# An encoder block in fp32 on one core: the first half's index queries for 128 tokens, in plain fp32

## The chip, the cores and the metric

The kernel runs on one core of a Trainium2 chip. A core has a matrix engine (TensorE, PE in the profile; its weight loads are shown as PEld), a vector engine (VectorE, DVE), a scalar engine (ScalarE, ACT), GpSimd (POOL), a queue engine that only starts transfers (SyncE, SP) and 16 DMA engines. Each engine works through its own instructions in order; they wait for one another by semaphores. The metric is the device time of one execution in microseconds (us), less is better.

## The reference

One layer for 512 tokens of width 2048, in fp32: a normed input is projected by one wide matrix `w_in`, two attention branches run on parts of the projection, their gated sum is added to the input, and a mixture-of-experts step (PEER) follows. What matters here is the index branch. It decides for each token which keys the sparse attention (DSA) may look at:

```python
h = rmsnorm(x, norm_mix_g[l])
proj = jnp.einsum('bsd,de->bse', h, w_in[l])
c_q, c_kv, k_rope, dq, dk, dv, iq, ik, iw, gates = jnp.split(proj, splits, axis=-1)
...
q_idx = rope(q_idx.reshape(B, S, IDX_HEADS, IDX_DIM), positions, IDX_ROT)      # 16 heads of 64
k_idx = rope(k_idx[:, :, None, :], positions, IDX_ROT)[:, :, 0, :]
top_k = min(DSA_TOPK_MAX, S // 4)                                              # 128
# for each block of 128 queries:
dots = jnp.einsum('bqhd,bsd->bqhs', qi_blk, k_idx).astype(jnp.float32) * IDX_DIM ** -0.5
index_score = jnp.einsum('bqh,bqhs->bqs', w, jax.nn.relu(dots))
index_score = jnp.where(allowed[None], index_score, NEG_INF)
_, sel = lax.top_k(index_score, top_k)
```

The first block of 128 tokens sees at most 128 keys, so all of them are chosen, whatever its index scores are.

## The kernel before

The 512 tokens are worked in two halves of 256 columns (HB), each of two blocks of 128 (P). For each half, `projections` lays the input out as 16 slices of k (KT), [128 x 256] each, and makes the projection in output chunks of 128 rows; `attention`, `branches` and `residual` follow. The expert step for both halves comes after, with gathers on POOL and DVE running beside the second half. A scheduler orders the instructions of each engine beforehand, by program order, priorities (weight loads go first) and a simulated time line; on the chip the order is fixed.

Precision comes from splitting. `wload` brings a weight tile of 128x1024 from memory (`raw`, 4 buffers, on SP's queue), ACT rounds it to `hi` (L114) and DVE makes the rest `lo` (L115); the input stands as `hT` and `lT` alike (L435, L437). `mm3` (L140 to L142) makes one product in three matmuls: hi by hi, hi by lo, lo by hi. `xraw` brings a weight tile without splitting it, for plain fp32 matmuls; the second half already uses that for its upper eight slices (`hF`, L386).

`proj_chunk(m)` is one output chunk of 128 rows for the 256 tokens of the half: two weight tiles, 16 slices, 48 matmuls of 256 columns in the first half. `scaled` multiplies the result by the row norms `rrow` (L397). The order of chunks in a half is: one for the keys (W_KRIK), two gates, eight of index queries (W_IQ), six latent ones, ten for the sparse attention's keys and queries, thirty gates.

The norms come out of the same loop that fills hT: ACT squares each slice (L440), DVE adds them up (L442), PE sums over partitions (L466), DVE and ACT make the reciprocal root (L148 to L154). PE can work two chunks ahead, the `pm` buffers, before the first scaled result `xk` must be taken out.

Each chunk m of index queries holds two heads of 64 rows. It is scaled, turned by position (`rope_near`: a shuffle, two products and a sum on DVE), and split by `stacked`: two ACT casts into `two` (L347), a DVE subtraction into `cq[1]` (L348), and two small transfers on SP's queue (L349, L350) that put the lower parts into the other 64 partitions. `cq[0]` has slots for two chunks (m % 2), `cq[1]` for four (m % 4). For each head and each block in `looks` then come two score matmuls against the keys (L354, L355), a Relu on ACT (L511) and a weighted sum on DVE into `sel` (L512). `looks` leaves block 0 out, so in the first half only block 1 is scored, though queries are made for both blocks. `tick` and `between` pace the gathers and the expert search and do nothing in the first half.

Of the kernel before, what the change touches and what calls it, by code (L numbers as in the profile page):

```python
# [7 lines left out]
F32 = mybir.dt.float32  # L8
# [9 lines left out]
P = 128  # L18
S = 512
# [58 lines left out]
def emit(tc, a, out):  # L78
    nc = tc.nc
    R = dict(side="right")  # L80
    with ExitStack() as top:
# [36 lines left out]
        def xraw(src):  # L118
            with tc.high_priority():
                raw = wp.tile([P, 1024], F32, name="raw", tag="raw", bufs=4)[:, :flat(src)]  # L120
                nc.sync.dma_start(raw, src)
            return raw
# [209 lines left out]

        def rope_near(dst, src, cs, half, tp):

            sh = tp.tile([P, HB], F32, name="rt2", tag="rt2")
            nc.vector.stream_shuffle(sh, src, [i ^ half for i in range(32)])
            t1 = tp.tile([P, HB], F32, name="rt1", tag="rt1")
            nc.vector.tensor_mul(t1, src, cs[0])
            nc.vector.tensor_mul(sh, sh, cs[1])
            dst = sh if dst is None else dst  # L340
            nc.vector.tensor_add(dst, t1, sh)
            return dst

        def stacked(two, lo, src):

            for t in two:
                nc.scalar.copy(t, src)  # L347
            nc.vector.tensor_sub(lo, src, two[0].bitcast(F32))  # L348
            nc.sync.dma_start(two[0][64:, :].bitcast(F32), lo[:64, :].bitcast(F32))  # L349
            nc.sync.dma_start(two[1][:64, :].bitcast(F32), lo[64:, :].bitcast(F32))  # L350
# [9 lines left out]
        def projections(i, pj, own, between, tick):  # L360
# [4 lines left out]
            with ExitStack() as st:  # L365
# [3 lines left out]
                hT = hp.tile([P, ks, HB], F32R, name="hT")  # L369
                lT = hp.tile([P, ks, HB], F32R, name="lT")  # L370
                hF = hp.tile([P, KT - ks, HB], F32, name="hF") if ks < KT else None
                trig = hp.tile([P, 4, HB], F32, name="trig")
                rcol = hp.tile([P, 2], F32, name="rcol")
                rrow = hp.tile([P, HB], F32, name="rrow")
# [5 lines left out]
                def proj_chunk(m):  # L380
                    pm = ps.tile([P, S], F32, name="pm", tag="mm")[:, :HB]
                    for hf in range(2):
                        if 8 * hf >= ks:
                            w = xraw(a["win"][m, hf])
                            for j in range(8):
                                nc.tensor.matmul(pm, w[:, j * P:(j + 1) * P], hF[:, j, :], start=False, stop=j == 7)  # L386
                            continue
                        wh, wl = wload(a["win"][m, hf])
                        for j in range(8):
                            k = 8 * hf + j  # L390
                            mm3(pm, wh[:, j * P:(j + 1) * P], wl[:, j * P:(j + 1) * P],
                                hT[:, k, :], lT[:, k, :], k == 0, k == KT - 1)
                    between(m)
                    return pm

                def scaled(dst, pm):
                    tick(nc.vector.tensor_mul(dst, pm, rrow), 5.7)  # L397
                    return dst
# [27 lines left out]
                with tc.tile_pool(name=f"a{i}", bufs=1) as ap:  # L426
                    sq = dq[:, 3, :]
                    for k0, n in [(k, min(3, e - k)) for b_, e in ((0, ks), (ks, KT)) for k in range(b_, e, 3)]:
                        src = a["wdv"][:, k0 * 272:(k0 + n) * 272]
                        wh, wl = wload(src) if k0 < ks else (xraw(src), None)  # L430
                        for k in range(k0, k0 + n):
                            if k % 4 == 0:
                                xt = xraw(a["xt"][i, k // 4])
                            x_ = xt[:, (k % 4) * HB:(k % 4 + 1) * HB]
                            nc.scalar.activation(hT[:, k, :] if k < ks else hF[:, k - ks, :], x_, AF.Copy, scale=gmix[:, k:k + 1])  # L435
                            if k < ks:
                                nc.vector.scalar_tensor_tensor(lT[:, k, :], x_, gmix[:, k:k + 1], hT[:, k, :].bitcast(F32),  # L437
                                                               ALU.mult, ALU.subtract)
                            s2 = sq if k == 0 else dq[:, 4 + k % 4, :]
                            nc.scalar.activation(s2, x_, AF.Square)  # L440
                            if k:
                                nc.vector.tensor_add(sq, sq, s2)  # L442
                        if k0 == K_A:
                            if i == 0:
                                nc.sync.dma_start(fr, a["freq"])
                                nc.sync.dma_start(ident, a["cmat"][:, 0:P])
                            nc.sync.dma_start(kk.bitcast(I32), a["posr"][:, side])
                            nc.vector.tensor_copy(posf, kk.bitcast(I32))
                            angles(2)
                        for j, tb in enumerate(blocks):  # L450
                            ts_ = slice(j * P, (j + 1) * P)
                            for d_ in range(n):
                                k = k0 + d_
                                if k >= ks:
                                    nc.tensor.matmul(pd[j], hF[:, k - ks, ts_], wh[:, d_ * 272:(d_ + 1) * 272],
                                                     start=False, stop=k == KT - 1)
                                    continue
                                mm3(pd[j], hT[:, k, ts_], lT[:, k, ts_], wh[:, d_ * 272:(d_ + 1) * 272],
                                    wl[:, d_ * 272:(d_ + 1) * 272], k == 0, k == KT - 1)
                    if i == 0:  # L460
                        nc.sync.dma_start(cm, a["cmat"][:, P:6 * P].rearrange("p (j q) -> p j q", j=5))
                        nc.sync.dma_start(cmask, a["cmask"])
                        nc.sync.dma_start(gq, a["gqkv"])
                        nc.sync.dma_start(iota, a["iota"])
                    pr = ps.tile([P, S], F32, name="prr", tag="tr")[:, :HB]
                    nc.tensor.matmul(pr, ones, sq, start=True, stop=True)  # L466
                    rr = rstd_of(ap, pr, D, "r")
                    nc.vector.tensor_copy(rrow, rr)
                    for j in range(2):
                        dg = ap.tile([P, P], F32, name="dg")  # L470
                        nc.vector.tensor_mul(dg, rr[:, j * P:(j + 1) * P], ident)
                        nc.vector.tensor_reduce(rcol[:, j:j + 1], dg, AX.X, ALU.add)
                    for j, tb in enumerate(blocks):
                        rc = rcol[:, j:j + 1]
                        nc.scalar.copy(dvw[:, tb, :], pd[j])
                        nc.vector.tensor_scalar(dvw[:, tb, :256], dvw[:, tb, :256], rc, None, ALU.mult)
                        nc.vector.tensor_scalar(dvw[:, tb, 256:], dvw[:, tb, 256:], rc, 1.0 / 32.0, ALU.mult, ALU.mult)
# [14 lines left out]


                for m in range(8):
                    xi = tp.tile([P, HB], F32, name="xi")
                    scaled(xi, proj_chunk(W_IQ + m))
                    iq = rope_near(None, xi, cs[2], 8, tp)

                    two = [cq[0][:, 2 * (m % 2) + j, :] for j in range(2)]
                    stacked(two, cq[1][:, m % 4, :], iq)  # L500
                    for hh in range(2):
                        h = 2 * m + hh
                        for b in looks:
                            n = (b + 1) * P
                            qs = slice((b % 2) * P, (b % 2 + 1) * P)
                            pi = ps.tile([P, S], F32, name="pi", tag=("tr", "po")[turn[0] % 2])[:, :n]
                            mm_stacked(pi, two, hh, qs, *ik, n, True, True)
                            turn[0] += 1
                            o = 4 + 2 * (turn[0] % 2)
                            rl = dq[:, o:o + 2, :].rearrange("p h t -> p (h t)")[:, :n]  # L510
                            nc.scalar.activation(rl, pi, AF.Relu)  # L511
                            nc.vector.scalar_tensor_tensor(  # L512
                                sel[b], rl, dvw[:, b, 256 + h:257 + h], cmask[:, S - n:] if h == 0 else sel[b],
                                ALU.mult, ALU.add)
# [587 lines left out]
```

## Time and profile before

| | |
|---|---|
| time, median of 3 runs | 3625.94 us (3624.42 to 3628.35) |
| the profiled execution | 3632.17 us, span 3630.4 us |
| PE / PEld / DVE / ACT / POOL busy | 94% / 84% / 78% / 39% / 16% |
| mean granted TensorE clock | 0.972 |
| HBM traffic | 281 GB/s over the span |

The profile is of one execution; its times are from the start of the span. Busy times are unions, so two overlapping matmuls count once. [...]

### The profile page before, as it was taken

Reading aid. Unit: us, or ns where it says so; the run is one execution under the profiler, and the core shown is the slowest. Engines: PE = TensorE matmul, PEld = TensorE weight load, DVE = VectorE, ACT = ScalarE, POOL = GpSimd, SP = SyncE. Lnnn points to the kernel's source line nnn. Section 1 sums busy time; section 2 is a strip of 40 time slices with the busy share of each in tenths; the row PEclk is TensorE's granted clock in tenths of the full one; section 3 lists DMA queues with packets and bytes.
Section 4 is the critical chain, followed back from the end, with each engine's and each line's share of the span. In section 5 each row is a group of like instructions: output and inputs, shape, how many; then the busy total and the mean of one; then the engine's idle time right before and its main releaser. Section 6 shows DMA issues by size and latency. Waiting matters only on the chain.

```text
span 3630.4 us, 55449 instructions
## 1 busy us (share of the span) xinstructions
PE 3407.4 (94%) x20981; PEld 3054.9 (84%) x20981; DVE 2842.7 (78%) x4726; ACT 1434.0 (39%) x2171; POOL 595.6 (16%) x388
## 2 busy tenths in 40 slices
PE   8999999999889788879999999999999999999997
PEld 7999898777788678659999999998778787788786
DVE  7854565589998778768998787876878788789797
ACT  6444554543122353334345444453233223233233
POOL 0000000000112222220001111110322233233232
PEclk9999999999999999989999999999999999999999
DMA  6566357543799768876788988989989898999997
GB/s 200 171 199 204 110 172 241 163 161 122 279 366 389 275 235 300 338 281 217 263 295 303 333 333 321 335 324 332 344 318 350 311 349 332 356 353 348 348 351 285
DMA packets 282108, 1026.23 MB, mean 283 GB/s; under 512 B 29424, under 2 KB 98672, under 8 KB 228080
## 3 DMA queue, kind: packets, MB, share of 16 engines
q1 hardware_dynamic: 193136, 565.47, 45.0%
q0 software_dynamic: 55296, 402.68, 29.0%
q10 hardware_dynamic: 33408, 54.54, 4.0%
q8 instruction: 165, 2.70, 0.3%
q14 instruction: 103, 0.84, 0.1%
HBM read 960.71 MB, written 58.72 MB: 281 GB/s over the span
## 4 chain that ended last, share of the span: by engine, by line
PE 73%; DVE 11%; DMA 8%; issue 5%; ACT 2%; POOL 0%; SPq 0%; DVEq 0%; ACTq 0%; POOLq 0%
PE pv L141 8%; PE pv L142 8%; PE pv L140 8%; PE pu L142 6%; PE pu L140 6%; PE pu L141 6%; PE pm L140 5%; PE pm L142 5%; PE pm L141 5%; DVE r L269 3%; DMA gt<-g_d 2%; PE pg L877 2%; DVE lo L115 2%; PE pu L832 2%; DMA raw<-in_vd 1%
## 5 line engine op out<-in xcount | busy, mean ns | idle before, releaser
L114 ACT CAST hi<-raw 128x1024 fp32r<-128x1024 f32 (+1 forms) x852 | 889.9, 1048 | 1346.1 <-PE pv L142 296.8
L115 DVE TENSOR_TENSOR lo<-raw,hi 128x1024 fp32r<-128x1024 f32 (+1 forms) x852 | 1033.3, 1218 | 491.3 <-issue 124.4
L267 POOL DMA_INDIRECT r<-in_u,idx x256 | 366.3, 1431 | 2525.6 <-DVE dots L269 1406.7
L141 PE MATMUL pv<-lo,ch 128*128 128x512 f32 x1536 | 600.6, 394 | 24.3 <-DVE lo L115 24.3
L142 PE MATMUL pv<-hi,cl 128*128 128x512 f32 x1536 | 594.2, 393 | 0.0
L269 DVE CUSTOM_DVE_ANT_0 r<-r,h2g 128x2048 f32<-128x2048 f32 x256 | 582.4, 2284 | 11.0 <-DMA r<-in_u,idx 11.0
L140 PE MATMUL pv<-hi,ch 128*128 128x512 f32 x1536 | 540.6, 392 | 9.4 <-ACT hi L114 8.6
L140 PE MATMUL pu<-h2h,hi 128*128 128x256 f32 x1888 | 539.2, 286 | 8.2 <-ACT hi L114 8.2
L142 PE MATMUL pu<-h2h,lo 128*128 128x256 f32 x1888 | 532.6, 282 | 0.5 <-DVE lo L115 0.5
L141 PE MATMUL pu<-h2l,hi 128*128 128x256 f32 x1888 | 531.4, 282 | 0.0
L140 PE MATMUL pm<-hT,hi 128*128 128x256 f32 x1368 | 405.3, 296 | 28.6 <-DVE sg L397 16.5
L142 PE MATMUL pm<-hT,lo 128*128 128x256 f32 x1368 | 397.5, 291 | 9.8 <-DVE lo L115 9.7
L141 PE MATMUL pm<-lT,hi 128*128 128x256 f32 x1368 | 396.6, 290 | 0.0
L141 PEld LDWEIGHTS pv<-lo,ch 128*128 128x128 f32 x1536 | 292.0, 190 | 91.0 <-DVE lo L115 30.2
L140 PEld LDWEIGHTS pu<-h2h,hi 128*128 128x128 f32 x1888 | 357.4, 189 | 9.0 <-ACT hi L114 8.5
L141 PEld LDWEIGHTS pu<-h2l,hi 128*128 128x128 f32 x1888 | 357.5, 189 | 0.4
L142 PEld LDWEIGHTS pu<-h2h,lo 128*128 128x128 f32 x1888 | 356.8, 189 | 0.9 <-DVE lo L115 0.8
L140 PEld LDWEIGHTS pv<-hi,ch 128*128 128x128 f32 x1536 | 290.2, 189 | 72.0 <-ACT hi L114 10.3
L142 PEld LDWEIGHTS pv<-hi,cl 128*128 128x128 f32 x1536 | 291.7, 190 | 60.6
L280 POOL DMA_INDIRECT r<-in_v,idx x128 | 229.2, 1790 | 484.1 <-DVE hacc L282 396.4
L282 DVE SCALAR_TENSOR_TENSOR hacc<-r,dots,hacc 128x2048 f32<-128x2048 f32 x128 | 300.1, 2345 | 8.5 <-DMA r<-in_v,idx 8.4
L140 PEld LDWEIGHTS pm<-hT,hi 128*128 128x128 f32 x1368 | 266.7, 195 | 37.3 <-issue 21.5
(356 smaller groups left out, 5262.0 us busy)
## 6 DMA issues: line engine op xcount, KB each, us to landing
raw<-in_ut SPq DMA_DIRECT2D x256, 512.0 KB
raw<-in_vd SPq DMA_DIRECT2D x256, 512.0 KB
raw<-in_win SPq DMA_DIRECT2D x228, 512.0 KB
raw<-in_wbr SPq DMA_DIRECT2D x64, 512.0 KB
raw<-in_wo SPq DMA_DIRECT2D x64, 512.0 KB
g_d<-gs ACTq DMA_DIRECT2D x24, 1024.0 KB
gt<-g_d SPq DMA_DIRECT2D x8, 3072.0 KB
raw<-in_wq SPq DMA_DIRECT2D x32, 512.0 KB
```

Source lines behind the costliest of these rows:

```text
L114: nc.scalar.copy(hi, raw)
L115: latest[0] = nc.vector.tensor_sub(lo, raw, hi.bitcast(F32))
L140: nc.tensor.matmul(ps, wh, xh, start=first, stop=False)
L141: nc.tensor.matmul(ps, wh, xl, start=False, stop=False)
L142: nc.tensor.matmul(ps, wl, xh, start=False, stop=last)
L267: nc.gpsimd.indirect_dma_start(out=r, out_offset=None, in_=a["u"], in_offset=bass.IndirectOffsetOnAxis(ap=idx[b][:, j:j + 1], axis=0))
L269: nc.vector.tensor_tensor_reduce(out=r, in0=r, in1=h2g[b], scale=1.0, scalar=0.0, op0=ALU.mult, op1=ALU.add, accum_out=dots[b][:, j:j + 1])
L280: nc.gpsimd.indirect_dma_start(out=r, out_offset=None, in_=a["v"], in_offset=bass.IndirectOffsetOnAxis(ap=idx[0][:, j:j + 1], axis=0))
L282: nc.vector.scalar_tensor_tensor(acc, r, dots[0][:, j:j + 1], acc, ALU.mult, ALU.add)
L832: nc.tensor.matmul(pu, w[:, j * P:(j + 1) * P], h2f[:, j, :], start=False, stop=j == 7)
L877: end[0] = nc.tensor.matmul(pg[:, j], o2[:, j, :], og[:, j, :], start=True, stop=True)
```

## The change

In the first half (i = 0) the eight index-query chunks are made for block 1 alone. A new tile `h1` holds block 1's 128 columns of the normed input's 16 slices in fp32; ACT writes it in the loop that fills hT, one instruction of 128x128 for each slice. An index-query chunk of the first half then is 16 plain fp32 matmuls of 128 columns with unsplit weights (`xraw`), in place of 48 of 256 columns with split ones. Scaling, rope and the split into `two` are done on 128 columns. In the second half the slices come out as before.

```diff
--- before.py
+++ after.py
@@ -332,9 +332,10 @@
 
         def rope_near(dst, src, cs, half, tp):
 
-            sh = tp.tile([P, HB], F32, name="rt2", tag="rt2")
+            n = src.shape[1]
+            sh = tp.tile([P, HB], F32, name="rt2", tag="rt2")[:, :n]
             nc.vector.stream_shuffle(sh, src, [i ^ half for i in range(32)])
-            t1 = tp.tile([P, HB], F32, name="rt1", tag="rt1")
+            t1 = tp.tile([P, HB], F32, name="rt1", tag="rt1")[:, :n]
             nc.vector.tensor_mul(t1, src, cs[0])
             nc.vector.tensor_mul(sh, sh, cs[1])
             dst = sh if dst is None else dst
@@ -369,6 +370,8 @@
                 hT = hp.tile([P, ks, HB], F32R, name="hT")
                 lT = hp.tile([P, ks, HB], F32R, name="lT")
                 hF = hp.tile([P, KT - ks, HB], F32, name="hF") if ks < KT else None
+
+                h1 = hp.tile([P, KT, P], F32, name="h1") if i == 0 else None
                 trig = hp.tile([P, 4, HB], F32, name="trig")
                 rcol = hp.tile([P, 2], F32, name="rcol")
                 rrow = hp.tile([P, HB], F32, name="rrow")
@@ -433,6 +436,8 @@
                                 xt = xraw(a["xt"][i, k // 4])
                             x_ = xt[:, (k % 4) * HB:(k % 4 + 1) * HB]
                             nc.scalar.activation(hT[:, k, :] if k < ks else hF[:, k - ks, :], x_, AF.Copy, scale=gmix[:, k:k + 1])
+                            if i == 0:
+                                nc.scalar.activation(h1[:, k, :], x_[:, P:], AF.Copy, scale=gmix[:, k:k + 1])
                             if k < ks:
                                 nc.vector.scalar_tensor_tensor(lT[:, k, :], x_, gmix[:, k:k + 1], hT[:, k, :].bitcast(F32),
                                                                ALU.mult, ALU.subtract)
@@ -492,17 +497,27 @@
 
 
                 for m in range(8):
-                    xi = tp.tile([P, HB], F32, name="xi")
-                    scaled(xi, proj_chunk(W_IQ + m))
-                    iq = rope_near(None, xi, cs[2], 8, tp)
-
-                    two = [cq[0][:, 2 * (m % 2) + j, :] for j in range(2)]
-                    stacked(two, cq[1][:, m % 4, :], iq)
+                    cols = slice(HB - len(looks) * P, HB)
+                    xi = tp.tile([P, HB], F32, name="xi")[:, cols]
+                    if i == 0:
+                        pm = ps.tile([P, S], F32, name="pm", tag="mm")[:, :P]
+                        for hf in range(2):
+                            w = xraw(a["win"][W_IQ + m, hf])
+                            for j in range(8):
+                                k = 8 * hf + j
+                                nc.tensor.matmul(pm, w[:, j * P:(j + 1) * P], h1[:, k, :], start=k == 0, stop=k == KT - 1)
+                        nc.vector.tensor_mul(xi, pm, rrow[:, cols])
+                    else:
+                        scaled(xi, proj_chunk(W_IQ + m))
+                    iq = rope_near(None, xi, [t[:, cols] for t in cs[2]], 8, tp)
+
+                    two = [cq[0][:, 2 * (m % 2) + j, cols] for j in range(2)]
+                    stacked(two, cq[1][:, m % 4, cols], iq)
                     for hh in range(2):
                         h = 2 * m + hh
                         for b in looks:
                             n = (b + 1) * P
-                            qs = slice((b % 2) * P, (b % 2 + 1) * P)
+                            qs = slice(looks.index(b) * P, looks.index(b) * P + P)
                             pi = ps.tile([P, S], F32, name="pi", tag=("tr", "po")[turn[0] % 2])[:, :n]
                             mm_stacked(pi, two, hh, qs, *ik, n, True, True)
                             turn[0] += 1
```

## Rows read from the trace of the kernel before

**Rows 1.** The page: engines' busy us (share); PE's busy tenths in 40 slices

```profile
PE 3407.4 (94%) x20981; PEld 3054.9 (84%) x20981; DVE 2842.7 (78%) x4726; ACT 1434.0 (39%) x2171; POOL 595.6 (16%) x388
...
PE   8999999999889788879999999999999999999997
```

**Rows 2.** Stretches (us from the start): busy time by engine, clock, DMA

```profile
core 0: us, PE busy (x) PEld busy (x) DVE busy (x) ACT busy (x) POOL busy (x), PEclk, DMA share, GB/s
9.00:18.00 9.00, 8.76 (x56) 8.50 (x56) 9.00 (x26) 8.77 (x21) 0.00 (x0) 1.00 0.83 265
18.00:27.00 9.00, 7.60 (x59) 7.40 (x60) 8.50 (x17) 6.69 (x15) 0.00 (x0) 1.00 0.75 235
27.00:36.30 9.30, 9.30 (x79) 9.25 (x79) 7.62 (x15) 6.92 (x9) 0.00 (x0) 1.00 0.86 276
36.30:44.20 7.90, 0.50 (x5) 0.29 (x3) 6.69 (x16) 4.75 (x6) 0.00 (x0) 0.69 0.51 172
...
54.00:107.50 53.50, 53.50 (x414) 50.35 (x413) 40.40 (x79) 28.12 (x47) 0.00 (x0) 1.00 0.57 185
...
121.00:388.00 267.00, 265.39 (x2188) 263.74 (x2187) 166.82 (x269) 118.03 (x144) 0.00 (x0) 1.00 0.61 193
...
1100.00:1200.00 100.00, 93.56 (x560) 84.36 (x559) 77.73 (x85) 21.37 (x30) 22.28 (x23) 0.98 1.00 397
```

**Rows 3.** Line 397, two stretches: ns min/median/max, first to last start (us)

```profile
L397 DVE TENSOR_TENSOR xi<-pm,rrow x8: 414/416/421, 61.3 to 108.7; 128x256 f32<-128x256 f32 x8
...
L397 DVE TENSOR_TENSOR sg<-pm,rrow x16: 417/418/420, 211.3 to 297.7; 128x256 f32<-128x256 f32 x16
```

**Rows 4.** Line 168; timeline and critical chain (start us, us, what) of plain fp32

```profile
L168 PEld LDWEIGHTS ptr<-ident,h2g x64: 187/192/333, 654.6 to 672.0; 128*128 128x128 f32 x64
L168 PE MATMUL ptr<-ident,h2g x64: 270/275/421, 654.8 to 672.1; 128*128 128x128 f32 x64
...
669.52 2.84 PE L168 MATMUL ptr<-ident,h2g 128*128 128x128 f32 x24
...
749.07 3.45 PE pm L386 x16
```

**Rows 5.** ACT's scaled copies: timeline, line 435, a group (busy us, mean ns)

```profile
8.49 2.49 ACT L435 ACTIVATE hT<-raw,gmix 128x256 fp32r<-128x256 f32 x6
...
L435 ACT ACTIVATE hT<-raw,gmix x8: 492/494/495, 8.5 to 11.9; 128x256 fp32r<-128x256 f32 x8
...
L578 ACT ACTIVATE dg<-ident,mxs 128x128 f32<-128x128 f32 x64 | 25.1, 400 | 3.1 <-DVE mxs L576 3.0
```

**Rows 6.** Ahead of the scores: critical chain, a DVE group, timelines

```profile
30.38 4.76 DMA raw<-in_win
...
L471 DVE TENSOR_TENSOR dg<-ry,ident 128x128 f32<-128x128 f32 x4 | 1.1, 282 | 0.0
...
66.96 0.42 DVE L397 TENSOR_TENSOR xi<-pm,rrow 128x256 f32<-128x256 f32 x1
...
69.86 0.42 DVE L341 TENSOR_TENSOR rt<-rt,rt 128x256 f32<-128x256 f32 x1
...
71.42 0.47 SPq L349 DMA_DIRECT2D cqh<-cql  x1
71.94 0.59 SPq L350 DMA_DIRECT2D cqh<-cql  x1
...
387.79 3.10 DMA two<-qrl
...
778.24 1.89 DMA cqh<-cql
```

**Rows 7.** The second half's first scores: PE's timeline, the stretch behind

```profile
780.27 0.66 PE L354 MATMUL pi<-ikh,cqh 128*128 128x384 f32 x1 [3.64 <-DMA cqh<-cql]
...
780.30:789.00 8.70, 8.70 (x22) 5.45 (x23) 8.70 (x38) 3.65 (x7) 0.00 (x0) 0.50 0.39 122
```

**Rows 8.** Line 397, 40 to 45 us: the first scaled result

```profile
L397 DVE TENSOR_TENSOR xk<-pm,rrow x1: 417/417/417, 43.7 to 43.7; 128x256 f32<-128x256 f32 x1
```

## The prediction

> **What bounds the kernel now.** I first read the engines' busy time and the forty slices [rows 1]: TensorE (PE) is busy 94% of the span, VectorE (DVE) 78%, and PE is near full from the second slice on. A share over the whole span doesn't price an edit of one stage, so I then read the stretches of the first half by engine [rows 2]. The changed code has two places. In 54 to 107.5 us, the index queries of the first half, PE is busy 53.5 of 53.5 us at a granted clock of 1.00, while DVE has 40.4, ScalarE (ACT) 28.1 and the DMA engines are at a share of 0.57. From 121 to 388, the rest of the first half's projections, PE is busy 265.4 of 267. So for over 330 us PE alone sets the pace: what PE is spared in the query stage comes off the time when the projections end, and all later work stands relative to that. The other place is the start-up, where h1 is made. There ACT has 8.77 of 9 us (9 to 18), 6.69 of 9 and 6.92 of 9.3, DVE is as full, and PE then stands idle from 36.3 to 44.2 except for 0.5 us, because the row norms come late. In the start-up it is the chain through ACT, DVE and DMA that counts, not PE.
>
> **What is removed from PE.** One output chunk of a split projection is 48 matmuls of 256 columns (16 slices of k, three products each). What such a chunk costs is read where nothing else runs on PE: the scaled results of the gates follow one another from 211.3 to 297.7 us, 16 of them, so 86.4 / 15 = 5.76 us a chunk [rows 3]. In the query stage eight results lie between 61.3 and 108.7, so 47.4 / 7 = 6.77 us; the difference of about 1.0 us is the score matmuls (L354, L355) in between. They stay: the first half scored the second block alone before too.
>
> **What is added to PE.** Sixteen plain fp32 matmuls of 128 columns with a weight tile of their own each. The trace has that form in the turning of the blocks (L168: 128x128 weights, 128 columns, fp32). Its 64 records are for 2 blocks x 16 slices, so each matmul is recorded as two passes, and 24 passes in a row take 2.84 us, the last of them 0.275: (2.84 - 0.275) / 23 = 0.112 us a pass [rows 4]. A chunk is then 16 x 2 x 0.112 = 3.57 us in place of 5.76: 2.19 us less, and 8 x 2.19 = **17.5 us** for the stage. The same plain form at 256 columns takes 0.216 us a pass (3.45 us for 16) [rows 4], so it would cost 6.9 us a chunk: the gain comes from the halved width, and it is only there because the first block's queries were never used.
>
> [...]
>
> **What is removed beside PE.** Sixteen casts and sixteen subtractions of 128x1024, the narrower scaling, rope and split of the queries, and half the bytes of their little copies between partitions. All of it lies beside PE at its full 53.5 of 53.5 [rows 2]; I cost it at nothing. Pace and side work (tick, between) do nothing in the first half, since no expert is known then. The second half's slices come out as they were.
>
> **What is added at the start.** Sixteen ACT copies of 128x128 with a scale per partition. Six of the 256-wide copies (L435) take 2.49 us, one alone 0.494, so a step is (2.49 - 0.49) / 5 = 0.40, 0.09 under one's own duration; the 128x128 form with a scale lasts 0.40 (L578) [rows 5], so a step is about 0.31 and the sixteen are 5.0 us. ACT's idle time from 9 to 36.3 us is 0.23 + 2.31 + 2.38 = 4.9 us [rows 2], and an xt tile is now let go only after its four new copies. Bounds: 0 if all fall into idle time, 5 if all are in series, a little under zero if the new order happens to bring the norms forward. Twelve of them meet the stretch where ACT is 97% busy and pass their delay on to the lower parts on DVE; I take **3 us**, nearer to that row.
>
> **Two new couplings in the query stage.** First, the weight tiles stay taken until PE has read them, no longer until DVE has split them. Four tiles of half a chunk at (3.57 + 1.0) / 2 = 2.3 us each leave 3 x 2.3 = 6.9 us from issue to use; a weight load on the critical chain took 4.76 us [rows 6]. The stream itself rises from 185 GB/s to about 185 x 6.77 / 4.57 = 274, under the 397 GB/s that 1100 to 1200 us shows [rows 2]. Covered, with some 2 us to spare; when a load in SP's queue stands behind a copy that waits for DVE, that margin is what it eats. Second, the scores need the copy of the lower parts. From the end of a chunk: five DVE steps of 0.28 (128x128, L471), two ACT casts of at most 0.40, one DVE step of 0.28, two issues from 71.42 to 72.53, and a landing of 1.89 to 3.10: 5.5 to 6.7 us [rows 6]. A chunk with its scores is 4.6, so the scores of a chunk can't follow the next chunk as they stand; they must lie in the one after. The two slots of the queries allow that (the casts that reuse a slot come two chunks, 9.1 us, plus 1.4 later). Before, the copy of 71.94 belongs to a result scaled at 66.96: that chain took 5.6 us up to the end of its issue (72.53), the add at 69.86 having stood behind a split of 1.22 that is now gone, and PE waited for none of it. Bounds of the waits: 0, and per chunk 6.7 - 4.6 = 2.1, so 17 us in all. No such wait is seen in this stage and the first of the second half is a single one [rows 7], so I take **1.5 us**, near zero.
>
> **The sum.** -17.5 + 3 + 1.5 = **-13.0 us**. The profiled execution took 3632.2 us (span 3630.4); it would become 3619. It lies 6.2 us over the median of 3625.9, which holds the same work, so the median becomes **3613 us**.
>
> **The rivals.**
> 1. *Part of the gain is eaten in place.* The start-up takes its whole 5 us and the scores wait 0.5 to 1.1 us a chunk (4 to 9 us). For it: chain 6.7 against 4.6. Against it: the slots leave room. -17.5 + 5 + 4 to 9: 3617 to 3622.
> 2. *The scores wait a whole landing each time (slower).* The order on PE is fixed beforehand; if it lays a chunk's scores straight behind the next chunk, PE stands 6.7 - 3.57 = 3.1 us in each of eight chunks: 25 us for a gain of 17.5, and with the start-up +10.6, 3637. [...] It decides from a mean wait of (17.5 - 3) / 8 = 1.8 us a chunk.
> 3. *The weight loads come to the surface.* A load lasts 0.192 us against a pass of 0.112 [rows 4]. Were it not hidden, a chunk would be 32 x 0.192 = 6.1 us, 0.4 over the old one: 3626 + 3 + 3 = 3632. L168 loads a new tile for every matmul too and still steps at 0.112, so this has little for it. [...]
> 4. *A better order.* The start-up's copies hide and the fuller freedom on DVE and ACT moves a later wait forward: 3600 to 3608.
> 5. *The gain doesn't last.* Something later runs to a time of its own. I see none: the gathers, attention and all loads start on events of the stages before.
>
> **How the numbers follow.** Forecast, 3608 to 3618: 0.60. Rival 1: 0.18. Rival 2: 0.08. Rival 3: 0.03. Rival 4: 0.08. Rival 5: 0.03. From 3601 to 3625 lie the forecast, rival 1 and most of rival 4, about 0.84. What can be told from no change is about 0.2%, 7 us: faster is below 3618.7. Faster: 0.60 + 0.07 of rival 1 + 0.08 = 0.75; same: the rest of rival 1, rival 5 and a part of 3 = 0.15; slower: 0.10.
>
> **What would show it.** Right: index-query matmuls of 128 columns in two records each, 0.11 us apart; results of the stage 4.6 us apart; PE full through it at a clock of 1.00; the first scaled result (xk, before at 43.7 [rows 8]) about 3 us later; the last gate of the first half some 13 to 14 us earlier. Wrong: PE waiting for the copy of the lower parts or for a raw weight tile, a clock under 1.00 in the stage, the first result over 5 us later, or an equal gain at the end of the first half that is gone by the end of the kernel.

## The result, and the profile after

The changed kernel takes 3600.4 us (median of six executions, 3594.2 to 3606.6) beside 3622.5 for the kernel before: a ratio of 0.9928, interval 0.9911 to 0.9944. Run again it came to 3600.9 beside 3623.1, 0.9942 (0.9923 to 0.9962). So the change gives some 22 us, 0.6%, where 13 were forecast. The median lies 7.6 us under the range of 3608 to 3618; 3.4 of these come from the starting point, which six executions put at 3622.5 in place of 3625.9. The first profile of the changed kernel happens to be of its fastest execution (3594.2) and the profile before of a longer one than its median (3632.2), so the two spans, 3592.4 and 3630.4, lie 38 us apart. How much of that is the change is the first question.

The page of the changed kernel, which answers to [rows 1], hardly moves: PE has 27 us less to do.

```profile
PE 3380.0 (94%) x20853; PEld 3028.6 (84%) x20853; DVE 2818.4 (78%) x4710; ACT 1419.3 (40%) x2170; POOL 596.6 (17%) x388
...
PE   8999899899899888879999999999999999999997
```

The stretches that answer to [rows 2] say more (columns as there):

```profile
9.00:18.00 9.00, 8.12 (x41) 7.90 (x42) 9.00 (x26) 9.00 (x27) 0.00 (x0) 1.00 0.63 206
18.00:27.00 9.00, 7.52 (x52) 6.42 (x50) 6.97 (x16) 8.97 (x23) 0.00 (x0) 1.00 0.63 207
27.00:36.30 9.30, 7.73 (x60) 7.29 (x60) 8.17 (x13) 8.70 (x14) 0.00 (x0) 1.00 0.73 262
36.30:44.20 7.90, 6.73 (x54) 6.42 (x53) 7.90 (x22) 2.34 (x2) 0.00 (x0) 1.00 0.72 240
44.20:54.00 9.80, 9.80 (x84) 9.70 (x83) 7.41 (x24) 5.57 (x10) 0.00 (x0) 1.00 0.13 40
54.00:107.50 53.50, 52.77 (x402) 48.23 (x401) 32.69 (x94) 20.10 (x45) 0.00 (x0) 1.00 0.74 236
```

ACT is full from 9 to 27 us, with the sixteen copies. But PE, idle from 36.3 to 44.2 before, now works through most of that stretch, and the granted clock (a share of full speed), 0.69 there before, is 1.00. The DMA engines' share in the query stage rises from 0.57 to 0.74.

The matmuls of the query stage are as forecast. Line 508 is the new matmul, line 509 takes its result (timeline: start, us, what; line view: ns min/median/max, first and last start; the last row is a wait: us in total, times, longest):

```profile
50.61 10.43 PE L508 MATMUL pm<-h,raw 128*128 128x128 f32 x92
61.03 0.36 PE L355 MATMUL pi<-ikh,cqh 128*128 128x256 f32 x1
...
L508 PE MATMUL pm<-h,raw x256: 270/275/377, 50.6 to 86.8; 128*128 128x128 f32 x128
...
L509 DVE TENSOR_TENSOR xi<-pm,rrow x8: 283/292/292, 54.5 to 88.9; 128x128 f32<-128x128 f32 x8
...
63.00 0.29 DVE L509 TENSOR_TENSOR xi<-pm,rrow 128x128 f32<-128x128 f32 x1 [0.36 <-PE pm L508]
...
82.29 0.29 DVE L509 TENSOR_TENSOR xi<-pm,rrow 128x128 f32<-128x128 f32 x1
...
PE pi L355 <- DMA cqh<-cql: 0.7, 1, 0.7
```

92 passes in 10.43 us are 0.112 us each, the price taken from [rows 4], though each lasts 0.275 by its own record: they overlap; 256 records are two for each of 128 matmuls. From 63.00 to 82.29 the results follow one another by 4.82 us (four steps). The last row is all that PE waits for in the stage: 0.7 us, once, for the copy of the lower parts.

Where the lead is made is read at points that every profile has: the first scaled result xk, the first index result, the casts of kr that open attention, and the first load of hF that opens the second half (start in us; the last column is from there to the last sum of acc):

```
                        xk    first xi   kr      hF     hF to the end
before, first profile   43.7   61.3    379.1   721.3     2889.1
before, run again       43.8   60.4    378.1   719.3     2875.6
after, first profile    42.6   54.5    359.8   700.2     2872.2
after, run again        42.1   54.0    356.3   697.6     2880.4
```

Up to the second half a kernel repeats itself within 4 us; behind it two executions of one and the same kernel lie 8 (the changed one) and 13 us (the one before) apart, in the part where the gathers run. The lead at the second half's start is 19 to 24 us, and the medians differ by 22. The rest of the 38 us is the spread between executions of one kernel.

### The profile page after: what moved, and what is told of

The parts are those of the page before. It is cut to its first block, busy times and chain, and to the rows that moved or that the text cites. A ratio compares the mean times of both kernels' runs of the same rounds, so it can differ in the third digit from the quotient of the medians.

```text
span 3592.4 us, 55141 instructions
## 1 busy us (share of the span) xinstructions
PE 3380.0 (94%) x20853; PEld 3028.6 (84%) x20853; DVE 2818.4 (78%) x4710; ACT 1419.3 (40%) x2170; POOL 596.6 (17%) x388
## 4 chain that ended last, share of the span: by engine, by line
PE 72%; DVE 12%; DMA 9%; issue 4%; ACT 2%; SPq 0%; POOL 0%; ACTq 0%; DVEq 0%; POOLq 0%
PE pv L141 8%; PE pv L142 8%; PE pv L140 8%; PE pu L142 6%; PE pu L140 6%; PE pu L141 6%; PE pm L140 5%; PE pm L142 5%; PE pm L141 5%; DVE r L269 3%; DVE lo L115 3%; DMA gt<-g_d 2%; PE pg L892 2%; PE pu L847 2%; DMA raw<-in_vd 1%
## 5 line engine op out<-in xcount | busy, mean ns | idle before, releaser
L114 ACT CAST hi<-raw 128x1024 fp32r<-128x1024 f32 (+2 forms) x836 | 872.6, 1048 | 1353.6 <-PE pv L142 288.4
L115 DVE TENSOR_TENSOR lo<-raw,hi 128x1024 fp32r<-128x1024 f32 (+2 forms) x836 | 1014.4, 1218 | 480.7 <-issue 118.3
L140 PE MATMUL pm<-hT,hi 128*128 128x256 f32 x1240 | 368.2, 297 | 26.5 <-DVE xi L400 10.1
L142 PE MATMUL pm<-hT,lo 128*128 128x256 f32 x1240 | 361.5, 292 | 13.4 <-DVE lo L115 13.4
L141 PE MATMUL pm<-lT,hi 128*128 128x256 f32 x1240 | 358.8, 289 | 0.0
L140 PEld LDWEIGHTS pm<-hT,hi 128*128 128x128 f32 x1240 | 242.2, 195 | 35.1 <-issue 16.9
```

The lines of the kernel that those rows point to most:

```text
L114: nc.scalar.copy(hi, raw)
L115: latest[0] = nc.vector.tensor_sub(lo, raw, hi.bitcast(F32))
L140: nc.tensor.matmul(ps, wh, xh, start=first, stop=False)
L141: nc.tensor.matmul(ps, wh, xl, start=False, stop=False)
L142: nc.tensor.matmul(ps, wl, xh, start=False, stop=last)
```

## The experiments

Each was timed beside the kernel before on the same chip (the first two, e2_copies and e3_late on one chip, the other four on another); a ratio is to the kernel before, with its 95% interval.

**The kernel before, again (e0_before).** No edit.

> The kernel before, run again as it is, to see which stretches repeat and which don't. Both theories: the first scaled result xk near 43.7 us, the index queries' first result at 61.3, the start of attention at 378.8 and of the second half's first load of dq near 716, each within 0.5 us of the first profile, since nothing there waits for gathers. Theory A (all of the measured gain is made before the second half, the rest of the profile pair's 38 us is chance): behind 900 us, where the gathers run, this profile lies up to 10 us from the first one. Theory B (the second half gains too, because it starts otherwise): it lies within 2 us everywhere. Time 3618 to 3628.

Ratio 0.9998 (0.9986 to 1.001). xk, the first index result and kr lie within 1 us of the first profile, hF 2 us ahead, the end 15.5 us ahead: theory A, with a wider spread than its 10 us. A difference of under some 15 us behind 900 us, in one pair of profiles, says nothing.

**The changed kernel, again (e1_after).** No edit.

> The changed kernel, run again as it is. Both theories: first scaled result at 42.6 us, start of attention at 359.6, second half some 21 us ahead of the kernel before, each within 0.5 us. Theory A (gain made before the second half): the lead at the end of the kernel is 21 us give or take some 8, the lead grows or shrinks only where gathers run; time 3602. Theory B (second half gains 12 to 17 more by itself): lead 33 to 38 us at the end again, time 3590.

3600.9 us. Its profile ends 17 us ahead of that of e0_before, after a lead of 21.7 at hF. Theory A again: the second half gives nothing that can be told. The expected half microsecond was too narrow: kr came 3.5 us earlier than in the first profile of this kernel (more on that at the end).

**The copies alone (e2_copies).** The copies into h1 in the opening loop of the kernel before, read by nobody.

```diff
+                h1 = hp.tile([P, KT, P], F32, name="h1") if i == 0 else None
...
+                            if i == 0:
+                                nc.scalar.activation(h1[:, k, :], x_[:, P:], AF.Copy, scale=gmix[:, k:k + 1])
```

> The kernel before with the sixteen ACT copies into h1 added in the opening loop and nothing else; h1 is read by nobody. Theory 1, the forecast's (the copies lengthen the chain through ACT): first scaled result 3 us later, at 46.7, and the kernel 3 us slower, 3625.5. Theory 2 (the copies only push the row norms to another place in the order, which ends the 7.4 us idle of PE and the half clock behind it): first scaled result near 42.6, granted clock 1.00 from 36 to 54 us, first index-query chunk 3.5 us earlier, kernel 3 to 4 us faster, 3619.

3623.2 us, ratio 0.9997 (0.998 to 1.0013). This interval is some 12 us wide, so the time alone can't tell a cost of 3 us from none; the points can. xk comes at 43.3, the first index result at 60.4, kr at 377.7: the same as in e0_before or up to 0.5 us earlier. Neither theory holds as it stands: the copies, with the order that the scheduler makes around them, cost nothing and give next to nothing. They do hold PE up: in the kernel before it finished the two chunks that it can work ahead by 36.9 us, here by 41.3. But it then waited for xk in any case, 7.4 us before and 2.4 here. Why xk did not come later is told further down: the order of the start is not the old one.

**Why the changed kernel is ahead of the copies alone.** DVE's timeline of the two, just ahead of xk (start, us, what), and PE's first row behind xk. First e2_copies:

```profile
41.39 0.28 DVE L471 COPY rrow<-ry 128x256 f32<-128x256 f32 x1
41.59 0.28 DVE L474 TENSOR_TENSOR dg<-ry,ident 128x128 f32<-128x128 f32 x1
41.79 1.22 DVE L115 TENSOR_TENSOR lo<-raw,hi 128x1024 fp32r<-128x1024 f32 x1
42.93 0.42 DVE L411 SCALAR_TENSOR_TENSOR dq<-dq 128x256 f32<-128x256 f32 x1
43.26 0.41 DVE L398 TENSOR_TENSOR xk<-pm,rrow 128x256 f32<-128x256 f32 x1
...
43.73 1.01 PE L321 MATMUL prot<-xk,cm 128*128 128x256 f32 x2 [2.42 <-DVE xk L398]
...
44.20:54.00 9.80, 9.80 (x66) 9.43 (x65) 9.03 (x27) 5.37 (x8) 0.00 (x0) 0.84 0.35 117
```

The changed kernel:

```profile
41.86 0.29 DVE L473 COPY rrow<-ry 128x256 f32<-128x256 f32 x1
42.06 0.28 DVE L476 TENSOR_TENSOR dg<-ry,ident 128x128 f32<-128x128 f32 x1
42.27 0.42 DVE L413 SCALAR_TENSOR_TENSOR dq<-dq 128x256 f32<-128x256 f32 x1
42.60 0.42 DVE L400 TENSOR_TENSOR xk<-pm,rrow 128x256 f32<-128x256 f32 x1
...
43.07 0.70 PE L321 MATMUL prot<-xk,cm 128*128 128x256 f32 x2 [1.17 <-DVE xk L400]
```

The order of these two is the same but for one instruction: the split of 1.22 us at 41.79. It belongs to the first weight tile of the index queries. Loads go first and run four tiles ahead, so this tile is split while the row norms are still being made, and xk stands behind it. The change has no such split. PE's wait is 1.17 us in place of 2.42. Over 44.2 to 54 us the granted clock is 0.84 behind the longer one and 1.00 behind the shorter one; with 0.50 as the low value, as in [rows 7], 0.84 stands for about 3 us at it, (1 - 0.84) x 9.8 / 0.5, an estimate.

**That split, put back (e9_splits).** The changed kernel with cast and subtraction of the first index chunk's two tiles, unread.

```diff
                             w = xraw(a["win"][W_IQ + m, hf])
+                            if m == 0:
+                                with tc.high_priority():
+                                    hi = wp.tile([P, 1024], F32R, name="hi", tag="hi", bufs=4)
+                                    lo = wp.tile([P, 1024], F32R, name="lo", tag="lo", bufs=3)
+                                    nc.scalar.copy(hi, w)
+                                    nc.vector.tensor_sub(lo, w, hi.bitcast(F32))
```

> The changed kernel with the cast and the subtraction of the first index-query chunk's two weight tiles put back, their results unread. Theory S (the changed kernel's lead at the start comes from the first of these subtractions, which stood straight ahead of xk on VectorE): xk 1.2 us later than in the changed kernel, at 43.3, PE idle 2.4 us ahead of it in place of 1.2, granted clock 0.50 for one stretch of 3.4 us behind it, first index result some 2.5 to 3 us later than in the changed kernel, whole kernel 3 us slower than it, 3604. Rival (the copies into h1 made the lead by moving the row norms): xk and the time as in the changed kernel, 3601.

At the start all of theory S comes out (L511 is the split):

```profile
42.17 1.21 DVE L511 TENSOR_TENSOR lo<-raw,hi 128x1024 fp32r<-128x1024 f32 x1
43.31 0.41 DVE L413 SCALAR_TENSOR_TENSOR dq<-dq 128x256 f32<-128x256 f32 x1
43.64 0.41 DVE L400 TENSOR_TENSOR xk<-pm,rrow 128x256 f32<-128x256 f32 x1
...
44.11 0.93 PE L321 MATMUL prot<-xk,cm 128*128 128x256 f32 x2 [2.23 <-DVE xk L400]
...
44.20:54.00 9.80, 9.80 (x64) 9.40 (x65) 9.23 (x29) 3.38 (x7) 0.00 (x0) 0.83 0.05 18
```

xk is 1.0 and 1.5 us later than in the two profiles of the changed kernel, the first index result (57.1) 2.6 and 3.1, and kr (362.6) 2.8 us later than in the one that had the same pace of matmuls. The time of the whole kernel missed the expectation: 3599.6 us, ratio 0.9937 (0.9917 to 0.9958), no slower than the changed kernel. With executions of one kernel up to 22 us apart, 3 us don't show in a median of six; the cause is shown for the start, not for the total.

**Fewer splits ahead of xk (e8_order).** The changed kernel with the first two gates moved behind the index queries in the first half.

```diff
-                for f in range(GF):
+                first = 0 if i == 0 else GF
+                for f in range(first):
...
-                for f in range(GF, KT):
+                for f in range(first, KT):
```

> The changed kernel with the two gates of f = 0 moved behind the index queries in the first half, so that no gate weights are split ahead of xk. Theory S (VectorE's splits ahead of xk set the start): four subtractions of 1.2 us leave the stretch ahead of xk, xk comes 3 to 5 us earlier, at 37 to 39, the gates' 11.5 us on PE come later, and the first half ends 2 to 4 us earlier than in the changed kernel; 3597. Rival (the row norms' chain through ScalarE, its table loads and the square sums set xk): xk stays within 1 us of 42, PE runs out of work earlier, 2 to 4 us slower than the changed kernel, 3604.

xk comes at 37.3, 4.8 to 5.3 us earlier, for four splits of 1.22 less: with the opening loop as it is, DVE's work is what sets xk. But kr starts at 358.8 beside 359.8 and 356.3, and the time is 3597.7, 0.9934 (0.9917 to 0.9951): not to be told from the changed kernel. The reason is PE: after 30.5 us it stood only 1.2 us in the changed kernel, so an xk 5 us earlier had only that idle time to end.

**h1 made later, by POOL (e3_late).** The opening loop as before, h1 as the sum of hT and lT.

```diff
-                            if i == 0:
-                                nc.scalar.activation(h1[:, k, :], x_[:, P:], AF.Copy, scale=gmix[:, k:k + 1])
...
+                if i == 0:
+                    for k in range(0, KT, 4):
+                        nc.gpsimd.tensor_tensor(h1[:, k:k + 4, :], hT[:, k:k + 4, P:].bitcast(F32),
+                                                lT[:, k:k + 4, P:].bitcast(F32), ALU.add)
```

> The changed kernel with h1 not made by ACT in the opening loop but by four POOL additions of hT and lT ahead of the index queries. The index queries are then as narrow and plain as in the change, and the opening loop is the old one. Theory 1 (the copies cost 3 us, the queries gain more than forecast): faster than the changed kernel by 3 us, 3597. Theory 2 (the new order at the start gave 3.5 us): first scaled result again at 43.7, PE idle 7.4 us before it and at half clock behind it, slower than the changed kernel by 3 to 4 us, so 16 to 18 us under the kernel before, 3605.

3609.3 us, 0.996 (0.9946 to 0.9975): 8.4 us slower than the changed kernel. xk at 44.0, the first index result 3.4 to 3.9 us later than there, hF 2.4 and 5.0 later. PE waited 4.7 us ahead of xk, not 7.4, and the granted clock over 44.2 to 54 was 0.75. So this is theory 2's direction, but it is no clean undoing of the copies: POOL's sums ran inside the opening loop, from 11 to 31 us. The first split of the index queries is missing ahead of xk here too, and yet xk is no earlier than in the kernel before, since the row norms began later (table below). The remaining 3 to 6 us arise in the second half and stay unexplained.

**The width alone, plain (e4_wide).** Queries for both blocks again, 256 columns, plain fp32.

```diff
-                h1 = hp.tile([P, KT, P], F32, name="h1") if i == 0 else None
+                h1 = hp.tile([P, KT, HB], F32, name="h1") if i == 0 else None
...
-                                nc.scalar.activation(h1[:, k, :], x_[:, P:], AF.Copy, scale=gmix[:, k:k + 1])
+                                nc.scalar.activation(h1[:, k, :], x_, AF.Copy, scale=gmix[:, k:k + 1])
...
-                    cols = slice(HB - len(looks) * P, HB)
+                    cols = slice(0, HB)
...
```

> The changed kernel with both blocks' index queries made, 256 columns wide, in plain fp32 with unsplit weights; h1 is twice as wide. Forecast's reading: a pass of 256 columns takes 0.216 us, a chunk 32 x 0.216 = 6.9 us in place of 5.76, the query stage 9.2 us longer than before; the start about 3 us shorter as in the changed kernel, or 2 less for the wider copies: 3629. Rival (the gain comes from leaving the splits out, not from the width): no slower than the changed kernel by more than a few us, 3605.

3630.4 us, 1.002 (1.001 to 1.0031). The forecast's reading: the passes step at 0.216 us, kr starts 8.8 us later than in e0_before. Unsplit weights by themselves lose. xk came at 44.1, 1.5 and 2.0 us later than in the changed kernel: the sixteen copies are longer here, 0.49 us in place of 0.39, and that is passed on to xk.

**The width alone, split (e5_split).** Block 1 alone with the old three products, no h1.

```diff
...
-                            w = xraw(a["win"][W_IQ + m, hf])
+                            wh, wl = wload(a["win"][W_IQ + m, hf])
...
-                                nc.tensor.matmul(pm, w[:, j * P:(j + 1) * P], h1[:, k, :], start=k == 0, stop=k == KT - 1)
+                                mm3(pm, wh[:, j * P:(j + 1) * P], wl[:, j * P:(j + 1) * P],
+                                    hT[:, k, P:], lT[:, k, P:], k == 0, k == KT - 1)
```

> The kernel before with the index queries of the first half on block 1's 128 columns alone, still three products with split weights, and no h1. Reading 1 (a pass costs by its columns, so 128 cost half of 256): a chunk is 48 x 0.06 = 2.9 us, the stage 23 us shorter than before, 3600, as good as the change. Reading 2 (a pass with a weight load of its own costs about 0.112 us at 128 columns, whatever it computes, as the score products of attention with 128 columns step): 48 x 0.112 = 5.4 us, the stage 3 us shorter, 3620; the change's gain then comes from 32 passes in place of 48.

3618.8 us, 0.9989 (0.9973 to 1.0005), kr 2.9 us earlier than in e0_before: reading 2. PE's timeline in the stage:

```profile
59.74 0.27 PE L141 MATMUL pm<-lT,hi 128*128 128x128 f32 x1
59.85 0.28 PE L142 MATMUL pm<-hT,lo 128*128 128x128 f32 x1
59.96 0.28 PE L140 MATMUL pm<-hT,hi 128*128 128x128 f32 x1
60.08 0.27 PE L141 MATMUL pm<-lT,hi 128*128 128x128 f32 x1
```

Starts 0.11 us apart, where 256 columns took 0.12: halving the width of the split products saves next to nothing. The change needs both of its parts: 32 passes of 0.112 in place of 48 of 0.120.

## Why the prediction was right or wrong, point by point

**What bounds the kernel.** Right for the query stage: PE full before and after, and what it was spared arrived at kr and at the end. For the start it named the right chain, ACT, DVE and DMA, but not which part of it sets which time (below).

**The price on PE.** Right. 5.76 to 3.57 us a chunk was forecast, from L168 [rows 4]; 92 passes gave 0.112 us each. The two kernels between agree: e5_split, 48 passes of 128 columns, was expected at 3620 and took 3618.8; e4_wide, 32 of 256, was expected at 3629 and took 3630.4. That weight loads come to the surface (rival 3) did not happen: loads of 0.19 us, passes 0.112 apart, 128 matmuls long.

**The two new couplings.** Right and small: 1.5 us forecast, 0.7 and 0.2 us of waiting seen in the two profiles. The results follow one another by 4.82 us, not 4.6, because the forecast's 1.0 us for a chunk's scores was read too low: 6.77 is a mean over seven intervals, and the first of them, 61.3 to 66.96 [rows 3, rows 6], is 5.7 long and holds no scores. The other six are (108.7 - 66.96) / 6 = 6.95, so the scores cost 1.2 us a chunk before, and 4.82 - 3.57 = 1.25 now. They stay, so little of the gain hangs on it: 6.95 - 4.82 = 2.13 us a chunk in place of 2.19. From xk to kr the changed kernel needs 317.2 us, e0_before 334.3; of these 17.1 us, 1.5 are the clock (an estimate: 3 us of work at half rate behind xk, from the 0.85 of e0_before over 44.2 to 54), which leaves 15.6 for the queries where 17.5 - 1.5 = 16.0 were forecast. Rivals 1 and 2, the scores waiting for their copies, did not come: the order laid them a chunk later, as the slots allow.

**The start, the step that failed.** The sum had +3 us. The runs show -2.7 against e0_before: xk 1.2 us earlier (42.6 beside 43.8) and an estimated 1.5 us from the clock, which stayed at 1.00 where e0_before had 0.85 over 44.2 to 54. Two statements were wrong.

The first is the price of the copies. They were set against ACT's idle time, as if the order around them stayed as it was. ACT was indeed filled, but the scheduler moved the casts and splits of the first weight tiles behind the opening loop, and the row norms ahead of them. Alone the copies moved xk and kr by half a microsecond (e2_copies), and the delay that they put on PE (4.4 us) went into its 7.4 us of idle time [rows 2]. The forecast had this case as its bound of "a little under zero if the new order happens to bring the norms forward", and took 3 us. The order is seen in the first step of the row norms on DVE (rv) and their reciprocal, here of the kernel before, the changed one and e4_wide:

```profile
35.00 0.42 DVE L148 TENSOR_SCALAR rv<-prr 128x256 f32<-128x256 f32 x1
38.05 1.75 DVE L150 RECIPROCAL ry<-ry 128x256 f32<-128x256 f32 x1 [1.17 <-ACT ry L149]
...
30.34 0.42 DVE L148 TENSOR_SCALAR rv<-prr 128x256 f32<-128x256 f32 x1
34.23 1.75 DVE L150 RECIPROCAL ry<-ry 128x256 f32<-128x256 f32 x1 [0.30 <-ACT ry L149]
...
31.71 0.42 DVE L148 TENSOR_SCALAR rv<-prr 128x256 f32<-128x256 f32 x1
35.77 1.75 DVE L150 RECIPROCAL ry<-ry 128x256 f32<-128x256 f32 x1 [0.30 <-ACT ry L149]
```

The same points in all ten profiles (starts in us; the last columns count the splits of 128x1024 that DVE has done by then):

```
                     rv     reciprocal  xk     reciprocal   splits ahead
                                               to xk        of rv, of xk
before, first       35.00   38.05      43.74     5.69          5, 7
before, again       36.26   38.12      43.80     5.68          5, 7
e5_split            35.55   37.35      43.03     5.68          5, 7
e3_late             37.67   39.47      44.02     4.55          5, 6
e2_copies           29.75   33.76      43.26     9.50          1, 7
e9_splits           30.32   34.13      43.64     9.51          1, 7
after, first        30.34   34.23      42.60     8.37          1, 6
after, again        29.81   33.72      42.09     8.37          1, 6
e4_wide             31.71   35.77      44.14     8.37          1, 6
e8_order            30.11   32.51      37.34     4.83          1, 2
```

With the copies the reciprocal starts some 4 us earlier, and more splits then stand between it and xk; the two nearly cancel. How early it starts hangs on ACT's opening loop: in e4_wide, with longer copies in the same order, all three points are 1.4 to 2.1 us later than in the changed kernel. So the copies do have a price, and the new order paid for it.

The second statement is under "what is removed beside PE": all splits were costed at nothing, as if they lay in 54 to 107.5 us. Nearly all of them do. The first tile's pair is done ahead of xk, and from the reciprocal to xk DVE's own work sets the time: one split less is 1.13 us less, 8.37 beside 9.50 and 4.55 beside 5.69. That is as much as xk's lead of 1.2 us. (Executions of one kernel differ by up to 0.5 us in xk, so the share of each of the two can't be told more finely.) The -1.5 of the clock took both, the copies' delay of PE and the missing split: PE's wait ahead of xk was 2.4 us with the copies alone and 4.7 without copies and split (e3_late), the clock over 44.2 to 54 being 0.84 and 0.75, and 1.2 in the changed kernel, with 1.00. These are the rows of the clock, e0_before and e3_late:

```profile
44.20:54.00 9.80, 9.73 (x63) 9.27 (x64) 8.51 (x28) 5.18 (x8) 0.00 (x0) 0.85 0.08 22
...
44.20:54.00 9.80, 9.51 (x55) 9.05 (x56) 7.67 (x28) 4.64 (x7) 0.00 (x0) 0.75 0.05 15
```

The row that would have told of the split was there: before, the critical chain (start, us, what) goes through one at 40.09, in the middle of the row norms' last steps. It is the seventh, the first of the index queries.

```profile
40.09 1.13 DVE lo L115
```

**The sum.** xk -1.2, clock -1.5, queries -15.6: -18.3, which is kr at 359.8 beside 378.1. In the pair of the second profiles it is 21.8; the medians say 22. The 3.5 us between these two pairs go with the pace of one execution's matmuls (below) and can't be put down to the change. Of the 9 us between forecast and result, 5.7 are thus the start; the queries gave 0.4 less than forecast, and 3 to 4 us stay open.

**Rival 4, a better order at the start,** was the case that came, and its range, 3600 to 3608, holds the result. The copies did hide, as it says; but it looked for DVE's freedom in a later wait, and not in the one split ahead of xk. That the median lies in the range is in part luck, as 3 to 4 us of the gain are not accounted for. **Rival 5** is out: the lead of the first half is the lead of the whole.

## What to carry to other kernels

When loads run ahead of their use, the work that a change removes does not all lie where its matmuls lie: find the first few of the removed instructions in the trace and see what stands behind them. What narrowing pays has to be read for each form of matmul: here it halved the plain passes (0.216 to 0.112 us) and did next to nothing for the split products (0.120 to 0.112), so those pay only when there are fewer of them. And where a scheduler makes the order, work that is added also moves other work: here the sixteen copies cost nothing, as the row norms went ahead of the weight splits, while with longer copies in the same order xk came 1.5 to 2 us later. So read the new order before a price is put on what is added.

## What was not expected of the hardware

A split product of 128 columns steps at 0.112 us, one of 256 at 0.120, though plain fp32 passes take 0.112 and 0.216 at the same widths.

The pace of the 256-column products wasn't the same in every execution. The two profiles of the changed kernel, over the same gates at a granted clock of 1.00, first and second:

```profile
200.00:300.00 100.00, 100.00 (x836) 100.00 (x835) 48.08 (x52) 43.37 (x52) 0.00 (x0) 1.00 0.66 207
```

```profile
200.00:300.00 100.00, 100.00 (x845) 100.00 (x844) 48.92 (x53) 44.38 (x53) 0.00 (x0) 1.00 0.67 208
```

A chunk took 5.76 us in the first and 5.70 in the second; e3_late also had 5.70, both profiles of the kernel before 5.76. For the plain passes of 128 columns no such difference was seen: the stage's score products, which they lie between, span 40.0 and 39.6 us, 0.7 and 0.2 of it waiting. The slower pace is 2.5 to 3 us over the first half, and its cause is open.

After the changed kernel's wait of 1.2 us ahead of xk the granted clock stayed at 1.00. After 2.42 us (e2_copies) and 2.23 (e9_splits) it was 0.84 and 0.83 over 44.2 to 54, by the estimate above about 3 us of the work behind at 0.50. In the kernel before's two waits of 7.4 us it fell while PE still stood (0.69 and 0.76 over 36.3 to 44.2; in the first profile it is 0.50 from 39.4 to 49.6), and by the same estimate it stayed low for 5.5 us of the work behind in one profile (0.72 over 44.2 to 54) and for 2.9 in the other (0.85): the same wait didn't cost the same each time. In the first profile the 256-column products step at 0.21 us up to 49.5 and at 0.12 from there.

```profile
44.20:54.00 9.80, 9.79 (x55) 9.33 (x56) 8.72 (x27) 5.24 (x8) 0.00 (x0) 0.72 0.06 17
```
